# The scan of a Mamba-2 layer: decays from running sums broadcast through DRAM, and the preceding chunks' part made feature-major

## The chip, the cores and the metric

One Trainium2 chip; the program runs on one of its cores. A core has a matrix engine (TensorE, PE in the profile, with its weight loads as PEld), a vector engine (VectorE, DVE), an activation engine (ScalarE, ACT), a general engine (GpSimd, POOL) and a queue engine (SyncE, SP). They run their instruction streams independently and wait for each other on semaphores. The metric is device time in microseconds (us); lower is better. Of each version several executions are timed and the median is taken; one more execution is recorded by the hardware profiler.

## What is computed

The kernel is a two-layer decoder trunk on 512 tokens with 1024 features: a Mamba-2 mixer and a convolutional feed-forward block, then differential attention and another feed-forward block. The change touches the state-space scan inside the Mamba-2 mixer alone. It has 32 heads of 64 features in 4 groups of 8 heads, a state of 128, and works on chunks of 128 tokens:

```python
def segsum(a):
    t = a.shape[-1]
    cs = jnp.cumsum(a, axis=-1)
    d = cs[..., :, None] - cs[..., None, :]
    mask = jnp.tril(jnp.ones((t, t), dtype=bool))
    return jnp.where(mask, d, -jnp.inf)

def ssd_chunked(xdt, a, bm, cm):
    ...
    a_cs = jnp.cumsum(ac, axis=-1)
    decay_in = jnp.exp(segsum(ac))
    cb = jnp.einsum('bclgn,bcsgn->bcgls', cc, bc)
    y_diag = jnp.einsum('bcgls,bgrcls,bcsgrp->bclgrp', cb, decay_in, xc)
    decay_states = jnp.exp(a_cs[..., -1:] - a_cs)
    states = jnp.einsum('bclgn,bgrcl,bclgrp->bcgrpn', bc, decay_states, xc)
    ...
    states_in = new_states[:, :-1]
    y_off = jnp.einsum('bclgn,bcgrpn,bgrcl->bclgrp', cc, states_in, jnp.exp(a_cs))
    return (y_diag + y_off).reshape(b, s, h, p)
```

`y_diag` is what the tokens of a chunk get from the same chunk: the products `cb` of C and B, times `decay_in`, the exponential of the difference of two running sums, for each head, masked to the past. `y_off` is what they get from the preceding chunks, through the states.

## The kernel before

The kernel is written with a tile framework: each engine's instructions are written in program order, and the framework derives the waits and puts each engine's instructions into a fixed order, in which independent pieces of work interleave. So on PE the blocks of large projections stand between the small products of the scan. Each engine then runs its own list strictly in order: an instruction that waits holds all that stands behind it on its engine.

**Large projections.** A float32 weight chunk of 512 KB is loaded on SP's queue (`emit_chunk`, L138), rounded by ACT to a high part `wh` (L148), and the rest `wl` is formed by DVE (L149). Both have three buffers, and loading runs two chunks ahead (`AHEAD`, L118). Each product is three matmuls in the fast type fp32r (`mm3`, L175 to L177), 24 of them for a block of 128 output features (`in_block`, L414), into one of four PSUM banks with the tag "mm". Small products use four other banks, with the tag "aux" (`aux_bank`, L60). In the profile `ps_in` is the input projection, `ps_o` the output projection of the mixer.

**The order of the mixer.** At its start the step sizes `dt` of all heads and chunks are made (L432 to L469), with tokens on the partitions and 128 columns, one for each chunk and head. `A` is dt times the negative decay rate (L474); `ah` and `al` are its fp32r part and the rest (L477, L478). Three fp32 products with triangular and all-ones matrices (`lt`, `ut`, `ones`, L480 to L482) give sums over the tokens of a chunk, and `dec` is their exponential: `dl` (the decay from a token to the chunk's end), `ea` (from the chunk's start to a token) and `et` (over the whole chunk).

Then, for each group `g` of 8 heads (L627): two blocks of convolution (`conv_block`, L421) give B and C with features on the partitions (`bT`, `cT`), four more give the features `xs` (4 tiles of 128 features by 512 tokens). The scan of the four chunks (`scan`, L598) is woven with the four blocks of the gate z (`z_blocks`, L590, through `weave`, L368). After it come the gate, the norm (`normed`, L611) and, one group later, the output projection (`out_proj`, L578).

**The scan of a chunk** (class `Chunk`, L490) has four steps:
- `tokens` (L526) transposes xs so that tokens stand on the partitions (L531), multiplies by dt to get `xd` (L533) and by `dl` to get `xe` (L536), and transposes B (`bt`, L538).
- `decays` (L502) makes `cb` (L506) and masks it (L508). For each half of the 8 heads POOL writes masked copies `rh` and `rl` of `ah` and `al` (affine_select, L515), and two fp32r products with `lt` add them up into the running differences for four heads, 128 by 512 (`sg`, L519 and L520). ACT takes the exponential (`m`, L522), DVE multiplies by `cb` (L523).
- `states` (L542): from chunk 1 on, C times the state `S` before this chunk gives `yo` with tokens on the partitions (L547), which DVE multiplies by `ea` (L549). Up to chunk 2, the product of bt and xe (`st`, L552) and the decayed state before it make the next state (L555 to L558).
- `outputs` (L560): for each of the four 128-feature tiles, two products of 64 columns, one for each head (L568), and from chunk 1 on a transpose of yo that is added in PSUM (L571). DVE then adds xs times the skip weight and writes back into xs (L575).

The chunks are staggered (L602 to L609): step t runs `tokens` and `decays` of chunk t, then `states` and `outputs` of chunk t − 1.

POOL has little else: parameter transfers at the start, one addition `gacc` for each group's norm (L652), and additions in the norm of the stream (L395).

Of the kernel before, what the change touches and what calls it, by code (L numbers as in the profile page):

```python
# [9 lines left out]
F32 = mybir.dt.float32  # L10
# [8 lines left out]
P = 128  # L19
# [5 lines left out]
NG = 4  # L25
# [14 lines left out]
def trunk_kernel(ctx: ExitStack, tc, x, ssm_ln_g, ssm_in_w, ssm_conv_w, ssm_conv_b, ssm_dt_bias,  # L40
# [19 lines left out]
    def aux_bank(name):  # L60
        return pp.tile([P, T], F32, tag="aux", name=name)
# [112 lines left out]
    def mm3(ps, wh, wl, xh, xl, start, stop):  # L174
# [10 lines left out]
    ut = cp.tile([P, P], F32, name="ut")  # L185
    pool.affine_select(out=ut, in_=ones, pattern=[[1, P]], compare_op=ALU.is_ge, fill=0.0,
                       base=0, channel_multiplier=-1)
# [225 lines left out]
    with tc.tile_pool(name="ssm_y", bufs=1) as yp, tc.tile_pool(name="ssm", bufs=1) as sp:  # L413
# [7 lines left out]
        def conv_block(j, key, dst):  # L421
            ps = in_block(key)
            w = lambda t: c1[:, t * 24 + j:t * 24 + j + 1]
            tmp = sp.tile([P, T], F32, tag="ctmp", name="ctmp%d" % j, bufs=2)
            act.activation(tmp, ps, AF.Identity, bias=c1[:, 96 + j:97 + j], scale=w(3))
            for s in range(1, 4):
                dve.scalar_tensor_tensor(out=tmp[:, s:], in0=ps[:, :T - s], scalar=w(3 - s),
                                         in1=tmp[:, s:], op0=ALU.mult, op1=ALU.add)
            act.activation(dst, tmp, AF.Silu)
# [35 lines left out]
        for n in (13, 11, 9, 7, 5, 3):  # L465
# [14 lines left out]
        pe.matmul(ps[:, 0:P], lt.bitcast(F32), A, start=True, stop=True)  # L480
        pe.matmul(ps[:, P:2 * P], ut, A, start=True, stop=True)
        pe.matmul(ps[:, 2 * P:3 * P], ones, A, start=True, stop=True)  # L482
# [7 lines left out]
        class Chunk:  # L490
# [10 lines left out]

            def decays(self):  # L502

                tag, cs = self.tag, self.cs
                ps = aux_bank("cb" + tag)
                pe.matmul(ps[:, :P], self.bT[:, cs], self.cT[:, cs], start=True, stop=True)  # L506
                cb = sp.tile([P, P], F32, tag="cb", name="cb" + tag, bufs=2)
                dve.tensor_tensor(out=cb, in0=ps[:, :P], in1=ut, op=ALU.mult)  # L508
                self.ms = []
                for q in range(2):  # L510
                    h4 = slice(self.hh.start + 4 * q, self.hh.start + 4 * q + 4)
                    rh = sp.tile([P, 4, P], F32R, tag="rh", name="rh%s_%d" % (tag, q), bufs=2)
                    rl = sp.tile([P, 4, P], F32R, tag="rl", name="rl%s_%d" % (tag, q), bufs=2)
                    for r, a in ((rh, ah.bitcast(F32)), (rl, al)):
                        pool.affine_select(out=r, in_=a[:, h4].unsqueeze(2).to_broadcast([P, 4, P]),  # L515
                                           pattern=[[0, 4], [1, P]], compare_op=ALU.is_ge, fill=0.0,
                                           base=0, channel_multiplier=-1)
                    ps = aux_bank("sg%s_%d" % (tag, q))
                    pe.matmul(ps, lt, fl(rh), start=True, stop=False)  # L519
                    pe.matmul(ps, lt, fl(rl), start=False, stop=True)  # L520
                    m = sp.tile([P, 4, P], F32, tag="m", name="m%s_%d" % (tag, q), bufs=4)
                    act.activation(fl(m), ps, AF.Exp)  # L522
                    dve.tensor_tensor(out=m, in0=m, in1=cb.unsqueeze(1).to_broadcast([P, 4, P]), op=ALU.mult)  # L523
                    self.ms.append(m)

            def tokens(self):  # L526

                tag, cs = self.tag, self.cs
                ps = aux_bank("xs" + tag)
                for b in range(4):  # L530
                    pe.transpose(ps[:, b * P:(b + 1) * P], self.xs[b][:, cs], ident)  # L531
                self.xd = sp.tile([P, HPG, 64], F32, tag="xd", name="xd" + tag, bufs=2)
                dve.tensor_tensor(out=self.xd, in0=byh(ps), in1=self.per_head(dt), op=ALU.mult)  # L533
                if self.c < NT - 1:
                    self.xe = sp.tile([P, HPG, 64], F32, tag="xe", name="xe" + tag, bufs=2)
                    dve.tensor_tensor(out=self.xe, in0=self.xd, in1=self.per_head(dl), op=ALU.mult)  # L536
                    ps = aux_bank("bt" + tag)
                    pe.transpose(ps[:, :P], self.bT[:, cs], ident)  # L538
                    self.bt = sp.tile([P, P], F32, tag="bt", name="bt" + tag, bufs=2)
                    act.activation(self.bt, ps[:, :P], AF.Copy)  # L540

            def states(self):  # L542

                tag, c = self.tag, self.c
                if c:
                    ps = aux_bank("yo" + tag)
                    pe.matmul(ps, self.cT[:, self.cs], fl(self.prev.S), start=True, stop=True)  # L547
                    self.yo = sp.tile([P, HPG, 64], F32, tag="yo", name="yo" + tag, bufs=2)
                    dve.tensor_tensor(out=self.yo, in0=byh(ps), in1=self.per_head(ea), op=ALU.mult)  # L549
                if c < NT - 1:  # L550
                    ps = aux_bank("st" + tag)
                    pe.matmul(ps, self.bt, fl(self.xe), start=True, stop=True)  # L552
                    self.S = sp.tile([P, HPG, 64], F32, tag="S", name="S" + tag, bufs=2)
                    if c == 0:
                        act.activation(fl(self.S), ps, AF.Copy)  # L555
                    else:
                        dve.tensor_tensor(out=self.S, in0=self.prev.S, in1=self.per_head(et), op=ALU.mult)
                        dve.tensor_tensor(out=self.S, in0=byh(ps), in1=self.S, op=ALU.add)  # L558

            def outputs(self):  # L560

                g, c, cs = self.g, self.c, self.cs
                ps = aux_bank("y" + self.tag)
                for b in range(4):
                    o = ps[:, b * P:(b + 1) * P]
                    for j in range(2):
                        h = 2 * b + j
                        pe.matmul(o[64 * j:64 * (j + 1), :], self.xd[:, h, :], self.ms[h // 4][:, h % 4, :],  # L568
                                  start=True, stop=(c == 0))
                    if c:  # L570
                        pe.matmul(o, fl(self.yo[:, 2 * b:2 * b + 2, :]), ident,  # L571
                                  is_transpose=True, start=False, stop=True)
                for b in range(4):
                    x_ = self.xs[b][:, cs]
                    dve.scalar_tensor_tensor(out=x_, in0=x_, scalar=c2[:, 64 + 4 * g + b:65 + 4 * g + b],  # L575
                                             in1=ps[:, b * P:(b + 1) * P], op0=ALU.mult, op1=ALU.add)

        def out_proj(g, yh, yl, norm):  # L578
            for c in range(4):
# [15 lines left out]
                zs.append(z)  # L595
                yield

        def scan(g, bT, cT, xs):  # L598
            cs = []
            for c in range(NT):  # L600
                cs.append(Chunk(g, c, bT, cT, xs, cs[-1] if cs else None))
            for t in range(NT + 1):  # L602
# [24 lines left out]
        for g in range(NG):  # L627
# [3 lines left out]
            conv_block(20 + g, "in%d" % (36 + g), cT)  # L631
            if g == 0:
                params_a()
            xs = []
            for b in range(4):
                t = sp.tile([P, T], F32, tag="xs", name="xs%d_%d" % (g, b), bufs=8)
                conv_block(4 * g + b, "in%d" % (16 + 4 * g + b), t)
                xs.append(t)
                if g == 1:
                    stream_in(b)  # L640
            zs = []
            weave(scan(g, bT, cT, xs), z_blocks(g, zs), 2, 3)
            acc = None
            for b in range(4):
                dve.tensor_tensor(out=xs[b], in0=xs[b], in1=zs[b], op=ALU.mult)
# [338 lines left out]
```

## Time and profile before

| | |
|---|---|
| median of 3 runs | 1417.81 us (1417.32 to 1417.83) |
| the profiled execution: its own time, its span | 1415.89 us, 1414.2 us |
| PE busy, PEld busy | 1396.2 us (99%), 1111.7 us (79%) |
| DVE busy, ACT busy, POOL busy | 896.0 us (63%), 660.8 us (47%), 111.7 us (8%) |
| moved by DMA | 125.50 MB, mean 89 GB/s |
| granted PE clock | 1.0 |

How to read the rows shown later. A row of the page's groups, and of the answers that group by line, has the source line, the engine, the operation, the output and input tiles, their shapes, and the count; then the summed time in us, the mean of one in ns, and the idle time of the engine just before these instructions with what ended it. A row of the timeline has the start in us from the span's start, the duration, the engine, the line and what it does; consecutive records of one kind are merged (x4). A fp32 matmul shows as two records, a fp32r matmul or a transpose as one. Matmuls are pipelined, so the duration of one overlaps the next, and what one costs is the distance between starts. A row of windows has the stretch, then the busy time of each engine in it with the number of instructions, the granted clock, the share of time in which the DMA engines were busy, and GB/s. The row of the chain "by line" gives the shares of the chain of work that ended last in one stretch.

### The profile page before, as it was taken

To read this page: it belongs to the slowest core of one execution; us is meant where nothing else is said; L and a number is where in the kernel's file an instruction comes from. 1 tells how busy PE (TensorE), PEld (TensorE's weight loads), DVE (VectorE), ACT (ScalarE), POOL (GpSimd) and SP (SyncE) were. 2 spreads that over 40 slices of the span, in tenths; PEclk is the share of its full clock that TensorE was granted. 3 is DMA by queue.
4 is the path that set the end of the run, shared out by engine and by line. 5 is a ranking of instruction groups with operands and counts; after the bars stand their busy time and mean duration, and the time that the engine had idled before them with its cause. 6 is when DMAs were issued, how large, how long until landed. Compare 5 with 4: busy or idle time off the path is not lost.

```text
span 1414.2 us, 16996 instructions
## 1 busy us (share of the span) xinstructions
PE 1396.2 (99%) x6518; PEld 1111.7 (79%) x6518; DVE 896.0 (63%) x1498; ACT 660.8 (47%) x1018; POOL 111.7 (8%) x123
## 2 busy tenths in 40 slices
PE   8999999999999999999999999999999999999998
PEld 6778688687787888888888887786778888888886
DVE  7767766667677777337764555756777775267742
ACT  6746535436344444124433456867655442234432
POOL 4310302202010000000001100000020000000000
PEclk9999999999999999999999999999999999999999
DMA  6224133132123333233323422222123332333232
GB/s 185 70 60 146 34 89 90 45 91 74 60 90 93 101 94 100 93 101 93 101 79 107 123 85 72 75 68 67 46 75 104 93 101 92 102 93 101 85 102 67
DMA packets 184902, 125.50 MB, mean 89 GB/s; under 512 B 6181, under 2 KB 176597, under 8 KB 184821
## 3 DMA queue, kind: packets, MB, share of 16 engines
q1 hardware_dynamic: 181312, 122.93, 28.9%
q10 hardware_dynamic: 2628, 1.15, 0.3%
q8 instruction: 51, 0.84, 0.2%
q0 software_dynamic: 880, 0.34, 0.1%
q14 instruction: 31, 0.25, 0.1%
HBM read 122.28 MB, written 2.12 MB: 88 GB/s over the span
## 4 chain that ended last, share of the span: by engine, by line
PE 85%; DVE 6%; ACT 5%; DMA 1%; issue 1%; POOLq 0%; POOL 0%; SPq 0%; ACTq 0%
PE ps_u L175 6%; PE ps_d L175 6%; PE ps_d L177 6%; PE ps_d L176 6%; PE ps_u L176 6%; PE ps_u L177 6%; PE ps_g L176 5%; PE ps_g L177 5%; PE ps_g L175 5%; PE ps_in L176 5%; PE ps_in L177 4%; PE ps_in L175 4%; PE ps_o L176 2%; PE ps_o L175 2%; PE ps_o L177 2%; PE y L568 1%
## 5 line engine op out<-in xcount | busy, mean ns | idle before, releaser
L176 PE MATMUL ps_g<-xgl,wh_g 128*128 128x512 f32 x352 | 137.2, 390 | 1.6 <-DVE xgl L319 1.6
L175 PE MATMUL ps_d<-hh,wh_d 128*128 128x512 f32 x352 | 137.5, 391 | 0.0
L177 PE MATMUL ps_d<-hh,wl_d 128*128 128x512 f32 x352 | 137.2, 390 | 0.0
L176 PE MATMUL ps_u<-xgl,wh_u 128*128 128x512 f32 x352 | 137.1, 390 | 0.0
L175 PE MATMUL ps_u<-xgh,wh_u 128*128 128x512 f32 x352 | 137.1, 390 | 0.0
L175 PE MATMUL ps_g<-xgh,wh_g 128*128 128x512 f32 x352 | 137.0, 389 | 0.1
L176 PE MATMUL ps_d<-hl,wh_d 128*128 128x512 f32 x352 | 137.0, 389 | 0.0
L177 PE MATMUL ps_u<-xgh,wl_u 128*128 128x512 f32 x352 | 137.0, 389 | 0.0
L177 PE MATMUL ps_g<-xgh,wl_g 128*128 128x512 f32 x352 | 136.9, 389 | 0.0
L175 PE MATMUL ps_in<-xgh,wh_in 128*128 128x512 f32 x320 | 127.5, 398 | 0.0
L176 PE MATMUL ps_in<-xgl,wh_in 128*128 128x512 f32 x320 | 126.6, 396 | 0.0
L177 PE MATMUL ps_in<-xgh,wl_in 128*128 128x512 f32 x320 | 126.1, 394 | 0.0
L149 DVE TENSOR_TENSOR wl_d<-wr_d,wh_d 128x1024 fp32r<-128x1024 f32 (+1 forms) x48 | 54.5, 1136 | 91.7 <-ACT wh_d L148 91.5
L148 ACT ACTIVATE wh_d<-wr_d 128x1024 fp32r<-128x1024 f32 (+1 forms) x48 | 47.5, 990 | 129.4 <-PE ps_d L176 115.3
L698 ACT ACTIVATE hh<-vg 128x512 fp32r<-128x512 f32 x44 | 27.8, 631 | 114.9 <-DVE vg L697 114.9
L681 DVE TENSOR_TENSOR uu<-ps_u,nr_f 128x512 f32<-128x512 f32 x44 | 30.4, 692 | 79.5 <-PE ps_u L177 79.5
L176 PEld LDWEIGHTS ps_g<-xgl,wh_g 128*128 128x128 f32 x352 | 66.1, 188 | 15.9 <-DVE xgl L319 2.3
L175 PEld LDWEIGHTS ps_g<-xgh,wh_g 128*128 128x128 f32 x352 | 66.0, 188 | 14.2 <-ACT xgh L318 0.5
L175 PEld LDWEIGHTS ps_u<-xgh,wh_u 128*128 128x128 f32 x352 | 66.1, 188 | 13.7
L177 PEld LDWEIGHTS ps_g<-xgh,wl_g 128*128 128x128 f32 x352 | 66.1, 188 | 13.7
L177 PEld LDWEIGHTS ps_u<-xgh,wl_u 128*128 128x128 f32 x352 | 66.1, 188 | 13.7
L177 PEld LDWEIGHTS ps_d<-hh,wl_d 128*128 128x128 f32 x352 | 66.1, 188 | 13.7
(315 smaller groups left out, 3013.3 us busy)
## 6 DMA issues: line engine op xcount, KB each, us to landing
wr_g<-in_ffn_up_w_dram SPq DMA_DIRECT2D x44, 512.0 KB, 3.7
wr_u<-in_ffn_up_w_dram SPq DMA_DIRECT2D x44, 512.0 KB, 3.8
wr_in<-in_ssm_in_w_dram SPq DMA_DIRECT2D x40, 512.0 KB, 3.8
wr_d<-in_ffn_down_w_dram SPq DMA_DIRECT2D x40, 512.0 KB, 3.3
wr_out<-in_ssm_out_w_dram SPq DMA_DIRECT2D x16, 512.0 KB, 3.5
wr_k<-in_kv_w_dram SPq DMA_DIRECT2D x8, 512.0 KB, 3.7
wr_q<-in_q_w_dram SPq DMA_DIRECT2D x8, 512.0 KB, 3.7
wr_v<-in_kv_w_dram SPq DMA_DIRECT2D x8, 512.0 KB, 3.8
```

Of the source, the lines that this page charges most:

```text
L148: act.activation(wh[:, :n], raw[:, :n], AF.Copy)
L149: dve.tensor_tensor(out=wl[:, :n], in0=raw[:, :n], in1=wh[:, :n].bitcast(F32), op=ALU.subtract)
L175: pe.matmul(ps, wh, xh, start=start, stop=False)
L176: pe.matmul(ps, wh, xl, start=False, stop=False)
L177: pe.matmul(ps, wl, xh, start=False, stop=stop)
L568: pe.matmul(o[64 * j:64 * (j + 1), :], self.xd[:, h, :], self.ms[h // 4][:, h % 4, :], start=True, stop=(c == 0))
L681: dve.tensor_tensor(out=u, in0=ps, in1=r, op=ALU.mult)
L698: act.activation(h, ga, AF.Copy)
```

## The change

The decays of a chunk no longer come from segment-sum products. The running sums of A over the tokens of each chunk, which the product with `ut` already makes, are kept as columns (`ccol`: tokens on partitions), and are also transposed by PE (`ps_cum`, `cumT`) and written by POOL's queue to a DRAM tile, with one row of 8 × 128 numbers for each chunk and group; their exponentials go to a second DRAM tile in the same way. For each chunk, a transfer on POOL's queue then broadcasts the row of sums to all 128 partitions (512 KB in SBUF). POOL subtracts each token's own sum and takes the minimum with zero, with one tensor_scalar instruction for each of the 8 heads, and ACT takes one exponential of 128 by 1024. The mask is that of `cb`, which zeroes what lies ahead of a token. From chunk 1 on, two more transfers broadcast the exponentials (`er`, 256 KB), one to each half of the partitions.

The part from preceding chunks is made with features on the partitions from the start: four products with slices of S as weights and C as the moving operand take the place of the one with C as weights. DVE multiplies them by `er` in place, and adds `er` to xs after `outputs`. The transposes of yo are gone. The tiles xs of a group become one tile of 128 by 4 by 512.

`decays` is split: the new `decays` holds the transfers, POOL's instructions and the exponential, `masked` holds cb and the product of m and cb. `decays` of chunks 0 and 1 is written ahead of the group's last convolution block, that of chunks 2 and 3 after `masked` of chunk 0.

```diff
-    lt = cp.tile([P, P], F32R, name="lt")
+    lt = cp.tile([P, P], F32, name="lt")
...
-        ah = sp.tile([P, NT * NH], F32R, name="ah")
-        al = sp.tile([P, NT * NH], F32, name="al")
...
-        dve.tensor_copy(ah, A)
-        dve.tensor_tensor(out=al, in0=A, in1=ah.bitcast(F32), op=ALU.subtract)
...
-        dl, ea, et = dec[:, 0:P], dec[:, P:2 * P], dec[:, 2 * P:3 * P]
+        dl, et = dec[:, 0:P], dec[:, 2 * P:3 * P]
+        split = lambda a: a.rearrange("p (i b j) -> p i j b", b=4, j=2)
+        rows = lambda a: a.rearrange("p (i j b) -> p i j b", j=2, b=4)
+        cum = sp.tile([P, 2, P], F32, name="cum")
+        ccol = sp.tile([P, P], F32, name="ccol")
+        dve.tensor_copy(ccol, ps[:, P:2 * P])
+        dve.tensor_copy(rows(cum[:, 0, :]), split(ps[:, P:2 * P]))
+        dve.tensor_copy(rows(cum[:, 1, :]), split(dec[:, P:2 * P]))
+        ps = aux_bank("ps_cum")
+        cumT = sp.tile([P, 2, P], F32, name="cumT")
+        cumd = [dp.tile([NT * NG, HPG * P], F32, name="cumd%d" % i) for i in range(2)]
+        for i in range(2):
+            pe.transpose(ps[:, i * P:(i + 1) * P], cum[:, i, :], ident)
+            dve.tensor_copy(cumT[:, i, :], ps[:, i * P:(i + 1) * P])
+            pool.dma_start(cumd[i].rearrange("i (q t) -> (i q) t", t=P), cumT[:, i, :])
...
             def decays(self):
...
+                i = self.c * NG + self.g
+                self.m = sp.tile([P, HPG, P], F32, tag="m", name="m" + self.tag, bufs=4)
+                pool.dma_start(self.m, cumd[0][i].partition_broadcast(P))
+                if self.c:
+                    self.er = sp.tile([P, 4, P], F32, tag="er", name="er" + self.tag, bufs=3)
+                    for j in range(2):
+                        half = slice(j * 4 * P, (j + 1) * 4 * P)
+                        pool.dma_start(self.er[64 * j:64 * (j + 1)], cumd[1][i, half].partition_broadcast(64))
+                for h in range(HPG):
+                    v = self.m[:, 4 * (h % 2) + h // 2, :]
+                    col = self.hh.start + h
+                    pool.tensor_scalar(out=v, in0=v, scalar1=ccol[:, col:col + 1], scalar2=0.0,
+                                       op0=ALU.subtract, op1=ALU.min)
+                act.activation(fl(self.m), fl(self.m), AF.Exp)
+
+            def masked(self):
+
+                cs = self.cs
+                ps = aux_bank("cb" + self.tag)
                 pe.matmul(ps[:, :P], self.bT[:, cs], self.cT[:, cs], start=True, stop=True)
...
-                self.ms = []
-                for q in range(2):
-                    h4 = slice(self.hh.start + 4 * q, self.hh.start + 4 * q + 4)
-                    rh = sp.tile([P, 4, P], F32R, tag="rh", name="rh%s_%d" % (tag, q), bufs=2)
-                    rl = sp.tile([P, 4, P], F32R, tag="rl", name="rl%s_%d" % (tag, q), bufs=2)
-                    for r, a in ((rh, ah.bitcast(F32)), (rl, al)):
-                        pool.affine_select(out=r, in_=a[:, h4].unsqueeze(2).to_broadcast([P, 4, P]),
-                                           pattern=[[0, 4], [1, P]], compare_op=ALU.is_ge, fill=0.0,
-                                           base=0, channel_multiplier=-1)
-                    ps = aux_bank("sg%s_%d" % (tag, q))
-                    pe.matmul(ps, lt, fl(rh), start=True, stop=False)
-                    pe.matmul(ps, lt, fl(rl), start=False, stop=True)
-                    m = sp.tile([P, 4, P], F32, tag="m", name="m%s_%d" % (tag, q), bufs=4)
-                    act.activation(fl(m), ps, AF.Exp)
-                    dve.tensor_tensor(out=m, in0=m, in1=cb.unsqueeze(1).to_broadcast([P, 4, P]), op=ALU.mult)
-                    self.ms.append(m)
+                dve.tensor_tensor(out=self.m, in0=self.m, in1=cb.unsqueeze(1).to_broadcast([P, HPG, P]), op=ALU.mult)
...
-                    pe.matmul(ps, self.cT[:, self.cs], fl(self.prev.S), start=True, stop=True)
-                    self.yo = sp.tile([P, HPG, 64], F32, tag="yo", name="yo" + tag, bufs=2)
-                    dve.tensor_tensor(out=self.yo, in0=byh(ps), in1=self.per_head(ea), op=ALU.mult)
+                    for b in range(4):
+                        pe.matmul(ps[:, b * P:(b + 1) * P], fl(self.prev.S[:, 2 * b:2 * b + 2, :]),
+                                  self.cT[:, self.cs], start=True, stop=True)
+                    dve.tensor_tensor(out=fl(self.er), in0=ps, in1=fl(self.er), op=ALU.mult)
...
-                        h = 2 * b + j
-                        pe.matmul(o[64 * j:64 * (j + 1), :], self.xd[:, h, :], self.ms[h // 4][:, h % 4, :],
-                                  start=True, stop=(c == 0))
-                    if c:
-                        pe.matmul(o, fl(self.yo[:, 2 * b:2 * b + 2, :]), ident,
-                                  is_transpose=True, start=False, stop=True)
+                        pe.matmul(o[64 * j:64 * (j + 1), :], self.xd[:, 2 * b + j, :], self.m[:, 4 * j + b, :],
+                                  start=True, stop=True)
...
+                if c:
+                    dve.tensor_tensor(out=self.xs[:, :, cs], in0=self.xs[:, :, cs], in1=self.er, op=ALU.add)
...
+        def scan(cs):
             for t in range(NT + 1):
                 if t < NT:
                     cs[t].tokens()
-                    cs[t].decays()
+                    cs[t].masked()
+                if t == 0:
+                    cs[2].decays()
+                    cs[3].decays()
                 if t:
                     cs[t - 1].states()
                     cs[t - 1].outputs()
                 yield
...
+            xs_ = sp.tile([P, 4, T], F32, tag="xs", name="xs%d" % g, bufs=2)
+            xs = [xs_[:, b, :] for b in range(4)]
+            cs = chunks(g, bT, cT, xs_)
             for b in range(4):
-                t = sp.tile([P, T], F32, tag="xs", name="xs%d_%d" % (g, b), bufs=8)
-                conv_block(4 * g + b, "in%d" % (16 + 4 * g + b), t)
-                xs.append(t)
+                if b == 3:
+                    cs[0].decays()
+                    cs[1].decays()
+                conv_block(4 * g + b, "in%d" % (16 + 4 * g + b), xs[b])
                 if g == 1:
                     stream_in(b)
             zs = []
-            weave(scan(g, bT, cT, xs), z_blocks(g, zs), 2, 3)
+            weave(scan(cs), z_blocks(g, zs), 2, 3)
```

More of the change, by code (lines that the diff above doesn't have):

```diff
@@ L476, in trunk_kernel @@
                                  op0=ALU.mult, op1=ALU.mult)
-        dve.tensor_copy(ah, A)
-        dve.tensor_tensor(out=al, in0=A, in1=ah.bitcast(F32), op=ALU.subtract)
         ps = aux_bank("ps_dec")
-        pe.matmul(ps[:, 0:P], lt.bitcast(F32), A, start=True, stop=True)
+        pe.matmul(ps[:, 0:P], lt, A, start=True, stop=True)
         pe.matmul(ps[:, P:2 * P], ut, A, start=True, stop=True)
@@ L506, in decays @@
+                for h in range(HPG):
[7 more added lines that the diff above has]
+                ps = aux_bank("cb" + self.tag)
                 pe.matmul(ps[:, :P], self.bT[:, cs], self.cT[:, cs], start=True, stop=True)
-                cb = sp.tile([P, P], F32, tag="cb", name="cb" + tag, bufs=2)
+                cb = sp.tile([P, P], F32, tag="cb", name="cb" + self.tag, bufs=2)
@@ L530, in tokens @@
                 for b in range(4):
-                    pe.transpose(ps[:, b * P:(b + 1) * P], self.xs[b][:, cs], ident)
+                    pe.transpose(ps[:, b * P:(b + 1) * P], self.xs[:, b, cs], ident)
                 self.xd = sp.tile([P, HPG, 64], F32, tag="xd", name="xd" + tag, bufs=2)
@@ L566, in outputs @@
                     for j in range(2):
[L567 to L572 removed]
+                        pe.matmul(o[64 * j:64 * (j + 1), :], self.xd[:, 2 * b + j, :], self.m[:, 4 * j + b, :],
+                                  start=True, stop=True)
                 for b in range(4):
[L574 removed]
+                    x_ = self.xs[:, b, cs]
                     dve.scalar_tensor_tensor(out=x_, in0=x_, scalar=c2[:, 64 + 4 * g + b:65 + 4 * g + b],
                                              in1=ps[:, b * P:(b + 1) * P], op0=ALU.mult, op1=ALU.add)
+                if c:
+                    dve.tensor_tensor(out=self.xs[:, :, cs], in0=self.xs[:, :, cs], in1=self.er, op=ALU.add)
         def out_proj(g, yh, yl, norm):
@@ L596, in z_blocks, with chunks @@
                 yield
-        def scan(g, bT, cT, xs):
+        def chunks(g, bT, cT, xs):
             cs = []
@@ L601, in scan @@
                 cs.append(Chunk(g, c, bT, cT, xs, cs[-1] if cs else None))
+            return cs
+        def scan(cs):
             for t in range(NT + 1):
```

3 lines of the change are left out of this document (removed).

## The prediction

> **What bounds the kernel now.** I read the busy times first, then the chain of work that ended last, then the windows of the four scans, one for each group of heads.
>
> ```profile
> PE 1396.2 (99%) x6518; PEld 1111.7 (79%) x6518; DVE 896.0 (63%) x1498; ACT 660.8 (47%) x1018; POOL 111.7 (8%) x123
> PE 85%; DVE 6%; ACT 5%; DMA 1%; issue 1%; POOLq 0%; POOL 0%; SPq 0%; ACTq 0%
> ```
>
> ```profile
> core 0: us, PE busy (x) PEld busy (x) DVE busy (x) ACT busy (x) POOL busy (x), PEclk, DMA share, GB/s
> 54.00:92.00 38.00, 38.00 (x205) 25.40 (x204) 26.50 (x50) 21.54 (x29) 16.57 (x17) 1.00 0.15 42
> 146.00:178.00 32.00, 31.17 (x170) 20.50 (x170) 22.31 (x42) 15.05 (x19) 11.82 (x12) 1.00 0.10 34
> 248.00:280.00 32.00, 32.00 (x176) 21.82 (x176) 20.43 (x40) 14.72 (x20) 9.94 (x9) 1.00 0.17 50
> 347.00:379.00 32.00, 31.90 (x173) 21.05 (x172) 21.32 (x41) 15.28 (x20) 5.64 (x5) 1.00 0.13 42
> sum 134.00, PE 133.07 PEld 88.77 DVE 90.57 ACT 66.59 POOL 43.97; mean PE 33.27 PEld 22.19 DVE 22.64 ACT 16.65 POOL 10.99
> ```
>
> TensorE (PE) is busy 133.07 of the 134 us of the scan windows. So a PE instruction taken out shortens the run, as long as no other engine runs out of room behind it. The mean window has 33.5 us, of which VectorE (DVE) works 22.64 (68%) and ScalarE (ACT) 16.65 (50%).
>
> **The change part by part.** Matmuls overlap, so I price them by the distance between starts. Here are three stretches of PE in group 0: the outputs of chunk 0, the segment sums and the preceding chunks' part of a chunk, and the outputs of that chunk.
>
> ```profile
> 65.02 1.09 PE L568 MATMUL y<-m,xd 128*64 128x128 f32 x16
> 66.04 0.66 PE L531 MATMUL xs<-ident,xs 128*128 128x128 f32 x4
> ...
> 77.31 0.48 PE L519 MATMUL sg<-rh,lt 128*128 128x512 f32 x1
> 77.63 0.40 PE L520 MATMUL sg<-rl,lt 128*128 128x512 f32 x1
> 77.86 0.39 PE L519 MATMUL sg<-rh,lt 128*128 128x512 f32 x1
> 78.09 0.40 PE L520 MATMUL sg<-rl,lt 128*128 128x512 f32 x1
> 78.33 1.02 PE L547 MATMUL yo<-S,cT 128*128 128x512 f32 x2
> 79.19 1.02 PE L552 MATMUL st<-xe,bt 128*128 128x512 f32 x2
> ...
> 80.37 0.44 PE L568 MATMUL y<-m,xd 128*64 128x128 f32 x4
> 80.74 0.33 PE L571 MATMUL y<-ident,yo 128*128 128x128 f32 x1
> 81.00 0.44 PE L568 MATMUL y<-m,xd 128*64 128x128 f32 x4
> ...
> 82.79 1.02 PE L547 MATMUL yo<-S,cT 128*128 128x512 f32 x2
> ```
>
> *Segment sums removed.* Four matmuls for each chunk, 77.31 to 78.33, take 1.02 us. The first start is 0.32 from the second, the others 0.23; that extra may pass to whatever f32r matmul follows the fp32 product cb, so I count 1.0. 16 chunks: 16.0 us (14.7 if all four are counted at 0.23).
>
> *Transposes of yo removed* (L571). With them a chunk's outputs run from 80.37 to 82.79, 2.42 us. Chunk 0, which has none, does the same eight products (16 records, two for each) in 66.04 − 65.02 = 1.02. So 1.40 us falls away in each of 12 chunks: 16.8 us. More than the transposes themselves goes, because the pairs of 64-column products then follow each other without a change of mode.
>
> *yo becomes feature-major.* One fp32 product with 512 columns (79.19 − 78.33 = 0.86) becomes four with 128 columns and four different weights. Two rows bound it:
>
> ```profile
> 36.99 0.39 PE L481 MATMUL ps_dec<-A,ut 128*128 128x128 f32 x2
> 37.21 0.39 PE L482 MATMUL ps_dec<-A,ones 128*128 128x128 f32 x2
> ```
>
> ```profile
> 101.29 1.05 PE L351 MATMUL tr_g<-ones,gacc 128*128 128x2 f32 x8
> 102.20 0.47 PE L177 MATMUL ps_in<-xgh,wl_in 128*128 128x512 f32 x1
> ```
>
> A fp32 128x128 product with weights of its own takes 0.22, so four take 0.88; four that are nothing but weight loads (2 columns) take 0.91. I take 0.91: 12 × 0.05 = 0.6 us more. The two transposes of the running sums cost under 0.33 (half of the 0.66 of the four at 66.04), once; I take 0.2.
>
> PE is therefore relieved of 16.0 + 16.8 − 0.6 − 0.2 = 32.0 us, 8 in each group, if everything else keeps pace (30.7 with the lower price of the segment sums).
>
> *What the other engines get.*
>
> ```profile
> L523 DVE TENSOR_TENSOR m<-m,cb 128x512 f32<-128x512 f32 x32 | 23.8, 768 | 3.4 <-ACT m L522 2.9
> L149 DVE TENSOR_TENSOR wl_in<-wr_in,wh_in 128x1024 fp32r<-128x1024 f32 x40 | 50.2, 1256 | 38.6 <-ACT wh_in L148 38.6
> L645 DVE TENSOR_TENSOR xs<-xs,z 128x512 f32<-128x512 f32 x16 | 10.7, 687 | 2.7 <-ACT z L594 2.7
> L186 POOL TENSOR_SCALAR_AFFINE_SELECT ut<-ones 128x128 f32<-128x128 f32 x1 | 0.3, 309 | 0.0
> L515 POOL TENSOR_SCALAR_AFFINE_SELECT rl<-al 128x512 fp32r<-128x512 f32 x32 | 35.3, 1104 | 0.0
> L652 POOL TENSOR_TENSOR gacc<-gsq,gsq 128x512 f32<-128x512 f32 x4 | 5.2, 1300 | 49.8 <-ACT gsq L647 49.8
> L246 POOL DMA_DIRECT2D sf<-in_ffn_conv_w_dram x12 | 6.4, 538 | 0.8 <-POOLq L969 0.8
> ```
>
> DVE: two products of m with cb (2 × 0.768) become one of 1024 columns (1.256 by the L149 row), 16 × −0.28 = −4.5 us; the new sum xs + er is 12 × 0.687 = 8.2; the multiplication by the decay stays, on another operand. Five copies at the start cost at most 5 × 0.687 = 3.4 less two small ones removed. About +1.2 us in each group's scan: 23.8 us of DVE in a window of 33.5 − 8 = 25.5, or 93%. That cover is thin. With DVE this full, some products will wait for it; I charge 1 us a group, 4 us in all.
>
> ACT: the exponentials have the same number of elements, now read from SBUF, and no more table loads than the 16 there are; its 16.65 us in 25.5 leave room.
>
> POOL: the affine selects go. Eight tensor_scalar of 128x128 for each chunk come, with one or three DMA issues. No row shows that operation. From below, the same shape costs 0.309 (L186); from above, POOL's dearest, a two-input 128x512, costs 1.300 (L652). I take 0.4, near the row of the same shape, with something for sharing with DVE. One chunk then needs 3 × 0.54 (issues) + 3.2 = 4.8 us of POOL, and its transfer a landing:
>
> ```profile
> tr<-bd SPq DMA_DIRECT2D x8, 256.0 KB, 3.5
> s2t<-in_lam_vecs_dram POOLq DMA_DIRECT2D x1, 128.0 KB, 4.7
> ```
>
> The first row is 128 partitions reading overlapping pieces of one 2.5 KB row of DRAM, so reading one row many times isn't slow in itself; the second is a broadcast from POOL's queue. I take 4.7 for 512 KB too (3.5 and twice 4.7 as ends). The added 16 × 512 + 12 × 256 KB are 11.5 MB in windows where the DMA engines are 10 to 17% busy. So POOL supplies a chunk in s = 4.7 + 4.8 = 9.5 us at the slowest, when no transfer overlaps the work of the chunk before.
>
> What queues behind a wait: on POOL, a tensor_scalar that waits for its transfer holds the next chunk's issues and the sum gacc; on ACT, an exponential that waits for POOL holds the casts wh of the weights, for which DVE and then PE wait. PE has the blocks of z and the projections meanwhile, with three weight buffers. In groups 1 to 3 the first transfers need only a free buffer of the group before, so they lie beside the convolutions. In group 0 they start from ps_dec at 37.2: sums to DRAM by about 46 (dec, copies, transposes, 0.54 and a landing), then 9.5 for chunk 0, exponential and product by about 58, against the first outputs at 65 now, some 61 later on. Chunks 1 to 3 follow each 4.8 to 9.5 later, against about 6.5 that the scan then takes for each. I charge 2 us here.
>
> The sum: 32.0 − 4 − 2 = 26 off the profiled execution of 1415.89 (its span 1414.2 and 1.7 around it): 1389.9. The median of the runs, 1417.81, stands 1.9 above that execution, so I forecast 1391 (rounded from 1391.8).
>
> **A rule that speaks against it.** Here POOL works beside a wide DVE instruction, and then without it:
>
> ```profile
> 38.14 1.62 POOL L515 TENSOR_SCALAR_AFFINE_SELECT rl<-al 128x512 fp32r<-128x512 f32 x1
> 39.72 0.63 POOL L515 TENSOR_SCALAR_AFFINE_SELECT rh<-ah 128x512 fp32r<-128x512 f32 x1
> ```
>
> The same shape takes 1.62 or 0.63, so POOL does wait for somebody. The Trainium skill ("SBUF — State Buffer", section "SBUF: two separate sides") says that GpSimd and DVE share a port pair as an exclusive lock, and that a DMA from the GpSimd queue is held up when DVE's two-port instructions keep GpSimd from writing its descriptors. The trace agrees for compute; no row here shows it for a descriptor. By that rule, applied to every issue of the change, the case "nothing is left" below would hold; by the 0.54 us row alone, the sum above.
>
> **Rivals.**
>
> *All of the gain.* If DVE keeps pace at 93%, 1417.8 − 32 = 1386. For it: PE is busy 133.07 of 134 us although DVE hands it work throughout. Against: it never had to at that density.
>
> *DVE becomes the bound of the scans.* The last group's chain already runs through DVE and ACT:
>
> ```profile
> by line: PE y L568 9.9%; PE ps_in L176 8.9%; DVE m L523 8.2%; PE ps_in L177 7.9%; PE ps_in L175 7.8%; PE y L571 7.4%; ACT L522 6.3%; PE yo L547 4.2%; DVE wl_in L149 4.0%; ACT L429 3.1%; ACT L594 3.1%; ACT m L522 2.9%; DVE xs L575 2.7%; issu
> ```
>
> If DVE can't go beyond 80%, a window takes 23.8 / 0.8 = 29.8, which saves 3.7 a group, 15 in all: 1403.
>
> *Nothing is left.* If each issue on POOL waits for one wide DVE instruction (three times 1.26), s grows to 13.3. Chunks 2 and 3 are asked for only when the scan starts; chunk 3 is needed three quarters into 25.5, at 19 us, and comes at 2s = 26.6: 7.6 us of PE idle in each group, 30 in all: 1416, no change.
>
> *Slower: POOL's arithmetic.* With p for one tensor_scalar, s = 6.3 + 8p, and a group loses 2s − 19. That passes the 8 us gained at s = 13.5, p = 0.9. At the 1.10 of the rl row, s is 15.1, the loss 11.2 × 4 = 45, and the time 1417.8 − 32 + 45 = 1431. For it: POOL's stretched rows. Against: 0.309 for the same shape, and blocks of the next group that PE may pull forward.
>
> **How the numbers follow.** Forecast (1391) 0.43, all of the gain 0.18, DVE bound 0.24, nothing left 0.05, slower 0.10. About 0.2%, 2.8 us, is what a measurement here can tell from no change. So faster 0.85, same 0.05, slower 0.10. The range goes from 1381 (all of the gain, and 5 us for prices that I rounded upwards) to 1411 (DVE bound, with half of what separates it from nothing left).
>
> **What would show it.** PE's busy time falls by about 30 us, rows sg and L571 are gone, a chunk's eight output products take about 1.0 us in every chunk and its four yo products about 0.9. POOL's tensor_scalar shows about 0.4, the broadcast lands within 5 us. Scan windows shorten by 6 to 8 us with DVE near 90%. Wrong would be: PE idle in the scans, released by m (DVE) or behind it by the exponential, POOL or the transfer; a tensor_scalar near 1 us; outputs that still take over 2 us.

## The result, and the profile after

The change made the kernel slower: 1469.6 us (1467.17 to 1471.87, 4 runs) against 1417.82, a ratio of 1.0365 (95% interval 1.0346 to 1.0385). I had forecast 1391. The profiled execution has a span of 1470.2 us, 56.0 more than before.

The page of the changed kernel: busy times; and the rows of PE, of POOL and of the granted PE clock in 40 equal slices of the span.

```profile
PE 1384.9 (94%) x6480; PEld 1118.6 (76%) x6480; DVE 895.1 (61%) x1497; ACT 648.9 (44%) x996; POOL 178.3 (12%) x229
...
PE   8774986996999999999999999999999999999998
...
POOL 4645062062001000000000200000020000000000
PEclk9986997997999999999999999999999999999999
```

PE was busy in 1396.2 of 1414.2 us; now it has holes in the first quarter of the span, and its clock falls with them. PE's idle time went from 18.0 to 85.3 us. Its busy time fell by only 11.3 us, though the same PE program without holes (the last experiment below) is busy for 1367.0 us: the 17.9 us more here are matmuls at a lower clock. In 84:88, where the granted clock is 0.50, one matmul of a projection starts 0.43 us after the other, and in 98:103, where it is 1.00, 0.23:

```profile
86.54 0.63 PE L176 MATMUL ps_in<-xgl,wh_in 128*128 128x512 f32 x1
86.97 0.63 PE L177 MATMUL ps_in<-xgh,wl_in 128*128 128x512 f32 x1
...
101.12 0.39 PE L177 MATMUL ps_in<-xgh,wl_in 128*128 128x512 f32 x1
101.35 0.40 PE L175 MATMUL ps_in<-xgh,wh_in 128*128 128x512 f32 x1
```

So 56.0 = −29.2 (work removed) + 17.9 (lower clock) + 67.3 (idle). Windows of four holes:

```profile
core 0: us, PE busy (x) PEld busy (x) DVE busy (x) ACT busy (x) POOL busy (x), PEclk, DMA share, GB/s
54.00:88.00 34.00, 16.59 (x63) 12.85 (x62) 9.86 (x13) 12.71 (x15) 23.28 (x33) 0.77 0.24 74
107.00:140.00 33.00, 12.78 (x60) 10.31 (x58) 9.44 (x15) 13.35 (x20) 24.22 (x33) 0.75 0.32 104
211.00:236.00 25.00, 8.64 (x34) 7.09 (x35) 12.27 (x21) 12.07 (x14) 17.57 (x21) 0.66 0.30 92
326.00:350.00 24.00, 8.41 (x30) 6.80 (x29) 7.69 (x16) 11.11 (x13) 13.98 (x19) 0.61 0.29 80
```

PE, DVE and ACT all idle more than half of each of these stretches; POOL alone is busy for more than half (58 to 73%). Who waits for whom in the changed kernel (total us, times, longest):

```profile
ACT m L529 <- POOL m L527: 75.8, 13, 8.3
PE tr_g L351 <- DVE gacc L674: 52.0, 3, 20.2
...
PE xs L545 <- ACT xs L429: 17.4, 2, 9.4
```

ACT waits 75.8 us for the decays m, PE does not. PE waits for xs, the last two silus of group 0's convolution (the first hole, 17.4 us), and for `tr_g`, the norm at the end of groups 0, 1 and 2 (the other three, 52.0 us): work of other kinds. What is late and what PE lacks are different things, and the timelines show how the one becomes the other. In the first hole it is group 0's own decays:

```profile
62.20 1.06 ACT L529 ACTIVATE m<-m 128x1024 f32<-128x1024 f32 x1 [6.00 <-POOL m L527]
...
64.57 0.63 ACT L429 ACTIVATE xs<-ctmp 128x512 f32<-128x512 f32 x1
...
65.25 0.69 PE L545 MATMUL xs<-ident,xs 128*128 128x128 f32 x2 [8.01 <-ACT xs L429]
```

The silu of one block of features stands in ACT's list behind the exponentials of chunks 0 and 1, and the last one, at 82.81, behind those of chunks 2 and 3; PE waits 8.01 and 9.39 us for them. At the end of group 0's scan it is the next group's decays (ACT and POOL):

```profile
94.97 1.28 ACT L529 ACT_TABLE_LOAD   x1 [3.39 <-DMA m<-cumd]
95.00 6.77 POOL L527 TENSOR_SCALAR m<-m,ccol 128x128 f32<-128x128 f32 x8 [3.54 <-DMA m<-cumd]
...
101.81 1.06 ACT L529 ACTIVATE m<-m 128x1024 f32<-128x1024 f32 x1 [5.55 <-POOL m L527]
102.88 1.28 ACT L607 ACT_TABLE_LOAD   x1
104.18 0.60 ACT L607 ACTIVATE z<-ps_in 128x512 f32<-128x512 f32 x1
104.67 1.05 ACT L148 ACTIVATE wh_in<-wr_in 128x1024 fp32r<-128x1024 f32 x1
105.75 1.28 ACT L529 ACT_TABLE_LOAD   x1
...
114.08 1.06 ACT L529 ACTIVATE m<-m 128x1024 f32<-128x1024 f32 x1 [7.04 <-POOL m L527]
```

All four chunks of group 0 have had their exponentials by 80.4 us. The two here are chunks 0 and 1 of group 1, and they stand in ACT's list ahead of group 0's gate z and of the casts wh of the next weights. ACT waits 5.55 and 7.04 us before them, with z and wh behind.

POOL's own rows, with the landing of the broadcast (median us):

```profile
L527 POOL TENSOR_SCALAR m<-m,ccol 128x128 f32<-128x128 f32 x128 | 105.0, 834 | 34.3 <-DMA m<-cumd 27.0 <-DVE er L564 4.3 <-DVE xs L667 2.7
```

```profile
m<-cumd POOLq DMA_DIRECT2D x16, 512.0 KB, 4.2
```

One tensor_scalar takes 0.834 us in the mean (0.707 in the median), where I had put 0.4. The transfer, at 4.2, is under the 4.7 that I took.

### The profile page after: what moved, and what is told of

The parts are those of the page before. It is cut to its first block, busy times and chain, and to the rows that moved or that the text cites. A ratio compares the mean times of both kernels' runs of the same rounds, so it can differ in the third digit from the quotient of the medians.

```text
span 1470.2 us, 17019 instructions
## 1 busy us (share of the span) xinstructions
PE 1384.9 (94%) x6480; PEld 1118.6 (76%) x6480; DVE 895.1 (61%) x1497; ACT 648.9 (44%) x996; POOL 178.3 (12%) x229
## 4 chain that ended last, share of the span: by engine, by line
PE 72%; DVE 5%; ACT 3%; POOL 2%; issue 1%; DMA 1%; POOLq 0%; ACTq 0%
PE ps_u L175 6%; PE ps_u L176 5%; PE ps_u L177 5%; PE ps_d L176 5%; PE ps_d L175 5%; PE ps_d L177 5%; PE ps_g L176 5%; PE ps_g L177 5%; PE ps_g L175 5%; PE ps_in L176 2%; PE ps_in L177 2%; PE ps_in L175 2%; POOL m L527 2%; PE ps_o L176 1%; PE ps_o L177 1%
## 5 line engine op out<-in xcount | busy, mean ns | idle before, releaser
L527 POOL TENSOR_SCALAR m<-m,ccol 128x128 f32<-128x128 f32 x128 | 105.0, 834 | 34.3 <-DMA m<-cumd 27.0
L176 PEld LDWEIGHTS ps_u<-xgl,wh_u 128*128 128x128 f32 x352 | 66.8, 190 | 14.0
```

Source lines behind the costliest of these rows:

```text
L176: pe.matmul(ps, wh, xl, start=False, stop=False)
L527: pool.tensor_scalar(out=v, in0=v, scalar1=ccol[:, col:col + 1], scalar2=0.0, op0=ALU.subtract, op1=ALU.min)
```

## The experiments

Every ratio is against runs of the kernel before on the same chip. Three theories stood at first. A (queue): ACT's list holds back the weight casts behind exponentials for which POOL is late. B (supply): the transfers through DRAM, or POOL's rate, make m itself late. C: the feature-major part costs more than it saves.

**POOL's subtractions left out.**

```diff
-                for h in range(HPG):
-                    ...
-                    pool.tensor_scalar(out=v, in0=v, scalar1=ccol[:, col:col + 1], scalar2=0.0,
-                                       op0=ALU.subtract, op1=ALU.min)
```

> The changed kernel with POOL's eight tensor_scalar instructions of each chunk left out, so that the exponential is taken of the broadcast sums themselves; transfers, exponentials and everything else stay. Theory A (queue): ACT stands ahead of exponentials whose input POOL has not finished (0.69 us for each tensor_scalar), and the weight casts behind them starve PE. Then PE's idle time of 85 us falls to about 20 and the time to 1385 to 1396. Theory B (supply): the transfers through DRAM and the buffers of m are what comes late. Then at least half of the loss stays, above 1440. Theory C (the feature-major part costs more than it saves): no change from 1470 beyond some 10 us.

Measured: 1398.4 us, ratio 0.9856 (0.9835 to 0.9877). The transfers stayed, so B in the form of slow transfers falls, and so does C. It is 2 us above what A gave; the wait of ACT for m is down from 75.8 to this, and is for the transfer now:

```profile
ACT m L524 <- DMA m<-cumd: 24.7, 9, 4.5
```

**The exponential late.**

```diff
             def decays(self):
...
-                act.activation(fl(self.m), fl(self.m), AF.Exp)
             def masked(self):
...
+                tc.keep_in_program_order(act.activation(fl(self.m), fl(self.m), AF.Exp))
                 dve.tensor_tensor(out=self.m, in0=self.m, in1=cb...
```

> The changed kernel with each chunk's exponential moved from its place right after POOL's instructions into the step of the scan that uses it, and pinned behind what ACT has before it there. POOL's work and the transfers are as they were. Theory A (queue): in groups 1 to 3 POOL has long finished by then, ACT no longer waits, PE idles only in group 0 and where the sum gacc stands behind POOL's tensor_scalar: 1390 to 1405. Theory B (supply): m is still late, PE and DVE wait for it instead: above 1440. Theory C: above 1450.

Measured: 1477.7 us, ratio 1.0411 (1.0396 to 1.0427): slower still, against A as it stood. But ACT no longer waits long for m. Waits of PE and ACT, then the timeline of this kernel:

```profile
ACT gsq L669 <- POOL gacc L674: 82.2, 4, 32.9
...
PE tr_g L351 <- DVE gacc L674: 78.4, 4, 31.9
```

```profile
93.98 1.14 ACT L669 ACTIVATE gsq<-xs 128x512 f32<-128x512 f32 x2
...
121.18 5.53 POOL L527 TENSOR_SCALAR m<-m,ccol 128x128 f32<-128x128 f32 x8 [2.36 <-DMA m<-cumd]
126.69 1.25 POOL L674 TENSOR_TENSOR gacc<-gsq,gsq 128x512 f32<-128x512 f32 x1
127.97 0.63 ACT L669 ACTIVATE gsq<-xs 128x512 f32<-128x512 f32 x1 [32.85 <-POOL gacc L674]
...
132.85 1.44 PE L351 MATMUL tr_g<-ones,gacc 128*128 128x2 f32 x6 [31.86 <-DVE gacc L674]
```

The two squares gsq are ready at 95, and POOL's one addition of them, 1.25 us long, starts at 126.69: it stands in POOL's list behind all four chunks of the next group. gsq has two buffers, so ACT can't go on to the third square, and the weight casts stand behind that. So there is a second queue of the same kind, on POOL itself. Theory A was refined: two lists hold urgent work behind the next group's decays.

**Each half of the change alone.** First the feature-major part with the segment sums of before (the new `states`, `outputs` and er with the old `decays`), then the new decays with yo transposed as before.

> The part from preceding chunks feature-major as in the changed kernel (with its transfers of er on POOL's queue), but the decays by segment-sum matmuls as before. Theories A and B: the 16.8 us of the transposes go, less 0.6 for the four products: 1400 to 1406. Theory C: 1418 or more.

> The decays from broadcast running sums as in the changed kernel, but the part from preceding chunks with tokens on the partitions and transposed, as before. Theories A and B: the segment sums' 16 us go, and the 88 us of PE idle time and slower clock that the changed kernel shows stay nearly whole: 1470 to 1495. Theory C: below 1425.

Measured: 1407.0 us, ratio 0.9910 (0.9894 to 0.9926), and 1455.7, ratio 1.0257 (1.0231 to 1.0282). The first is faster, so C falls; its PE is busy for 1383.0 us, 13.2 less. The second has the loss, though it lies 14 us below the range expected, and why is open: PE idles 54.6 us there (1456.7 − 1402.1) in place of 85.3. Its PE is busy for 1402.1 us, more than before although work was taken out, with a mean granted clock of 0.979.

**gacc on DVE alone, and with the late exponential.**

```diff
-                    (pool if b == 1 else dve).tensor_tensor(out=a2, in0=acc, in1=sq, op=ALU.add)
+                    dve.tensor_tensor(out=a2, in0=acc, in1=sq, op=ALU.add)
```

> The changed kernel with one edit: the sum gacc of each group's norm, which POOL did, goes to DVE; exponentials stay where the changed kernel has them. Theory A, refined by the run with the late exponential: two queues hold work back, ACT's behind the early exponentials and POOL's, where gacc stands behind the tensor_scalars of the next group. Then this takes away the second alone; ACT still waits for POOL before the exponentials: 1440 to 1465. Theory B (supply): what PE waits for is m; gacc makes no difference, 1465 to 1475. If gacc alone was it: below 1410.

> Both edits: the exponential pinned late as in the earlier run, and gacc on DVE. POOL's tensor_scalars and all transfers stay as slow as they are. Theory A (two queues): ACT and DVE wait no more for POOL in groups 1 to 3, PE idles a few us in group 0: 1388 to 1402. Theory B (supply): POOL needs 34 us for a group, PE still waits, for m: above 1430.

Measured: 1454.3 us, ratio 1.0254 (1.0231 to 1.0276), and 1392.7, ratio 0.9812 (0.9797 to 0.9826). The four combinations together:

| | gacc on POOL | gacc on DVE |
|---|---|---|
| exponential early | 1.0365 | 1.0254 |
| exponential late | 1.0411 | 0.9812 |

Either edit by itself leaves one of the queues standing. With gacc alone moved, PE still waits 16.3 us for xs and 38.4 for `tr_g`; with the exponential alone late, 3.2 and 78.4. Both together take nearly the whole loss away, with POOL's work and the transfers no quicker. The page of the combination, and POOL's subtractions in it:

```profile
PE 1367.6 (99%) x6480; PEld 1105.2 (80%) x6480; DVE 896.8 (65%) x1501; ACT 651.0 (47%) x996; POOL 184.7 (13%) x225
```

```profile
L527 POOL TENSOR_SCALAR m<-m,ccol 128x128 f32<-128x128 f32 x128 | 114.0, 904 | 48.9 <-DMA m<-cumd 48.7
```

They are even slower there (904 ns) and wait longer for transfers (48.7 us), and it costs little: PE waits 3.2 us for xs in group 0 and not for `tr_g`. B falls.

**The subtractions on DVE**, all eight with the order left to the framework, then four on each engine.

```diff
-                    pool.tensor_scalar(out=v, in0=v, scalar1=ccol[:, col:col + 1], scalar2=0.0,
+                    dve.tensor_scalar(out=v, in0=v, scalar1=ccol[:, col:col + 1], scalar2=0.0,
                                        op0=ALU.subtract, op1=ALU.min)
```

> The changed kernel with the eight subtractions of each chunk on DVE instead of POOL; order as the framework makes it, transfers on POOL. Theory A: the order is harmless as soon as what it takes for granted is quick; DVE has 8 x 0.23 us more for a chunk, some 29 us in all: 1390 to 1410. Theory B in the form that the transfers are the supply: above 1430. If DVE was the bound of the scans, as one of the rivals on record said: 1405 to 1420.

> The changed kernel with four of the eight subtractions of each chunk on POOL and four on DVE; nothing pinned, gacc on POOL. Theory A (two queues): POOL's share of a chunk falls from about 6.5 us to about 3, so that what stands behind it waits less: between the 1392 of all on DVE and 1470, nearer to the first, 1395 to 1425. If one of the two moves of work matters by itself and not the time POOL needs (DVE's larger share, say): 1450 or more, or 1392 at once.

Measured: 1392.0 us, ratio 0.9808 (0.9793 to 0.9822), and 1429.2, ratio 1.0078 (1.0053 to 1.0102). The first needs no pin: an order that sets the next group's work ahead does no harm when that work is quick (295 ns each on DVE, in this row of the groups of instructions).

```profile
L527 DVE TENSOR_SCALAR m<-m,ccol 128x128 f32<-128x128 f32 x128 | 30.7, 295 | 2.7 <-DMA m<-cumd 2.7
```

With half, about half of the loss comes back, (1.0078 − 0.9808) / (1.0365 − 0.9808) = 48%; the time lies a little above the range that I had expected. At this one point in between, what stands behind POOL waits about in proportion to POOL's work.

**POOL's work doubled in the good order.** Each subtraction of the combination is followed by a second tensor_scalar that caps its result.

> The version with the late exponential and gacc on DVE, with each subtraction on POOL followed by a second instruction of the same form, which caps its result (the decays are no longer the reference's). POOL then needs some 13 us for a chunk, 52 and the waits for transfers for a group of about 90. Theory A: groups 1 to 3 still have room, since nothing that PE needs early stands behind POOL; group 0, where the four chunks come one after another from 46 us on, waits for m some 20 to 30 us: 1405 to 1430. If POOL's time counts wherever it lies (theory B after all): four groups lose 26 us each, above 1470.

Measured: 1418.1 us, ratio 0.9999 (0.9985 to 1.0012), in the range of A. Windows of this kernel:

```profile
core 0: us, PE busy (x) PEld busy (x) DVE busy (x) ACT busy (x) POOL busy (x), PEclk, DMA share, GB/s
54.00:110.00 56.00, 33.27 (x188) 24.49 (x187) 25.03 (x45) 17.81 (x21) 50.95 (x68) 0.82 0.19 64
110.00:150.00 40.00, 39.86 (x184) 32.61 (x183) 28.13 (x49) 20.13 (x32) 33.16 (x42) 0.95 0.49 143
...
200.00:300.00 100.00, 99.11 (x507) 79.44 (x506) 74.71 (x128) 43.60 (x54) 75.61 (x92) 1.00 0.40 119
```

POOL has over 100 us more to do, and the kernel loses about 26 us, of which 22.7 are PE's idle time in group 0 (56.00 − 33.27). In 200:300 POOL works 76 of 100 us and PE idles 0.89. So in this order a slow POOL costs time in group 0 alone, where the sums first go to DRAM. PE's waits there:

```profile
PE xs L547 <- ACT xs L429: 14.4, 1, 14.4
PE y L584 <- DVE m L540: 7.8, 2, 5.6
```

The greater part was not expected in this form: for 14.4 us PE lacks not m but the convolution's last silu, which again stands in ACT's list behind an exponential (that of chunk 1, for which ACT waits 11.34 us).

**The price by itself.** Four forms of POOL's instruction in one kernel, two heads each.

> The price by itself: the changed kernel with POOL's eight instructions of a chunk in four forms, two heads each: subtract and minimum with a column as the scalar (as it is), minimum alone with a column, multiply and minimum with constants, minimum alone with a constant. The decays are then not the reference's. If the second operation is what costs, the one-operation forms take about 0.35 us and the others 0.7; if the column is, the constants take 0.35; if neither, all take 0.7, and 0.31 of the affine select was no guide to it. Time by theory A: between 1398 and 1470.

A single run took 1458.0 us. In order: as it is, minimum alone with a column, two operations with constants, minimum alone with a constant (count, min/median/max in ns):

```profile
L528 POOL TENSOR_SCALAR m<-m,ccol x32: 702/728/2115, 51.1 to 324.6; 128x128 f32<-128x128 f32 x32
```

```profile
L531 POOL TENSOR_SCALAR m<-m,ccol x32: 587/598/2580, 52.5 to 325.8; 128x128 f32<-128x128 f32 x32
```

```profile
L533 POOL TENSOR_SCALAR m<-m x32: 630/647/1540, 54.7 to 327.5; 128x128 f32<-128x128 f32 x32
```

```profile
L535 POOL TENSOR_SCALAR m<-m x32: 513/522/1237, 56.0 to 328.6; 128x128 f32<-128x128 f32 x32
```

The second operation adds 0.12 us and the column 0.07; even the plainest form takes 0.51 at the least. None comes near the 0.31 of the affine select of the same shape.

**Two more versions, both faster than the kernel before.** The combination with group 0's subtractions on DVE, and with all of them there.

> The version with the late exponential and gacc on DVE, with group 0's subtractions on DVE and those of the other groups on POOL. Theory A: what is left of the loss is in group 0, where POOL starts only after the sums have been to DRAM; 0 to 4 us less than the version with all on POOL: 1388 to 1393.

> The late exponential, gacc on DVE and all subtractions on DVE. Theory A: nothing waits for POOL any more, each of the two ways out is enough, and both together bring no more: 1388 to 1396. If DVE's room was short: above 1396.

Measured: 1388.7 us, ratio 0.9793 (0.9765 to 0.9820), and 1386.3, ratio 0.9772 (0.9748 to 0.9797). Their intervals overlap, and the first one's overlaps that of the combination (0.9797 to 0.9826), so what group 0 alone brings is not shown. The second, with everything off POOL but the transfers, has no PE wait over 1.2 us in the scans; a window in group 0's scan:

```profile
core 0: us, PE busy (x) PEld busy (x) DVE busy (x) ACT busy (x) POOL busy (x), PEclk, DMA share, GB/s
50.00:84.00 34.00, 33.26 (x192) 25.33 (x191) 30.74 (x75) 20.04 (x24) 5.27 (x10) 1.00 0.61 162
```

## Why the prediction was wrong

**The step that failed** is the paragraph on what queues behind a wait. It named the right objects: gacc behind POOL's tensor_scalars, and the casts wh behind an exponential. It then let them pass, because PE "has the blocks of z and the projections meanwhile, with three weight buffers", and because the decays of groups 1 to 3 "lie beside the convolutions". The runs showed that the framework sets the next group's decays into this group's scan, as soon as a buffer of m comes free, and so ahead of this group's gate and norm in two lists. That cost 52.0 us in the waits for `tr_g`. In group 0, for which I charged 2 us by the time at which m arrives, 17.4 us went to a wait for the convolution's silus, behind the group's own exponentials; with the exponential late it shrank to 3.2, with POOL no quicker. The cover counted on, z and the projections, is itself fed by the casts that stand in the blocked list. I read where `decays` stands in the code, and should have asked what ACT and POOL would have in front of wh and gacc.

**The price that fed it**, 0.4 us for a tensor_scalar, was half of the 0.834 measured. Of my two bounds, 0.31 and 1.30, I chose by shape, and the four forms of the operation take 0.51 to 0.70 at that shape. With 0.834 in the sum of the slower rival (s = 6.3 + 8 × 0.834 = 13.0, loss 4 × 7.0) I would have had 1414, not 1470: the rival had the right engine and a wrong place. It let PE wait for m of the group's own chunks 2 and 3; what PE waits for is the end of the group, behind the next group's decays, and in group 0 the convolution.

**The work removed from PE** was right in kind: 32.0 us forecast, 29.2 measured in the last version. The decays give 29.2 − 13.2 = 16.0, as forecast. The feature-major part gives 13.2 in place of 16.2. Its products, in chunks 1 and 2 of the changed kernel:

```profile
91.64 1.16 PE L562 MATMUL yo<-cT,S 128*128 128x128 f32 x8
92.63 1.02 PE L567 MATMUL st<-xe,bt 128*128 128x512 f32 x2
93.59 1.09 PE L582 MATMUL y<-m,xd 128*64 128x128 f32 x16
94.61 0.50 PE L177 MATMUL ps_in<-xgh,wl_in 128*128 128x512 f32 x1
...
96.76 1.05 PE L562 MATMUL yo<-cT,S 128*128 128x128 f32 x8
97.57 0.48 PE L177 MATMUL ps_in<-xgh,wl_in 128*128 128x512 f32 x1
```

The eight output products of a later chunk take 1.02 us from their first start to that of what follows (94.61 − 93.59), as forecast. The four of yo take 0.99 in one chunk and 0.81 in the next; in the last version the mean of all twelve is 0.90, against the 0.91 that I took. What I sized too large is what the transposes cost: 2.42 is the time of chunk 2 of a group, and chunks 1 and 3 take about 2.3, in two pieces. Over all 16 chunks the outputs go from 32.2 us to 16.4, which is 15.8 less and not 16.8. Most of the other 2 us is not in the scan: the products `warm` and `ps_dt` at the kernel's start take 1.8 us more in the execution profiled for this half; during `ps_dt` (16:20) the granted clock was 0.57 there, against 1.00 before. The last version shows the same there, by 1.6 us.

**The other charges.** 6 us were given back for DVE's density and group 0. With the queues cleared, the total stood at 1386.3 to 1392.7, around the forecast of 1391, and that is in part luck: in the combination PE's busy time fell by 28.6 us, not by 32, and its idle time rose by 2.8, not by 6. (By the terms of my own sum DVE's extra was 3.7 / 4 = 0.9 us a group, not 1.2; nothing hangs on it.) That DVE can't go beyond 80% is refuted: in the window above it works 30.74 of 34.00 us (90%) and PE still 33.26.

**The rule that I weighed**, the lock between GpSimd and DVE (the Trainium skill, "SBUF — State Buffer", section "SBUF: two separate sides"), agrees with the compute rows again: the same instruction takes 702 to 2115 ns. For descriptors these runs show no sign of it: an issue of m takes 0.583 us in the mean and its transfer lands in 4.2.

**The lower clock** was in none of my cases. In the holes the granted clock falls to 0.61 to 0.77, which made 67.3 us of idle time cost 17.9 more. The Trainium skill ("TensorE: Matmul & The Clock Gate", section "Why this matters for your kernels") asks for no idle gap above about 3 us between bursts of matmuls; the trace agrees, with waits of up to 20.2 us and those clocks.

## What to carry to other kernels

Work taken off the bounding engine pays only if what replaces it does not stand, in some other engine's list, in front of what feeds the bound. For each new instruction on an in-order engine, list what will be behind it, including work of the next iteration that an automatic order moves ahead; then take the price from a row of the same operation, not of the same shape. The tables of waits show it: where an engine waits long for something unrelated to the change, follow that wait to the list that it stands in.

## What the runs showed of the hardware

The shortest tensor_scalar on POOL took 0.51 us for 128 by 128 elements (one operation, a constant) and 0.70 in the form that the kernel uses (two operations, a column), against 0.31 for an affine select of the same shape on POOL and 0.295 (mean) for the kernel's form on DVE. Broadcasting one 4 KB row of DRAM to 128 partitions lands in 4.2 us for 512 KB, near the 3.8 of a weight chunk of that size.
